# Linear attention in octets of heads: the first octet's K is loaded in two transfers of 48 and 80 rows instead of one of 128

## The chip, the cores and the metric

The kernel runs on one core of a Trainium2 chip. The metric is the time of one execution in device microseconds; the median of several runs counts. The core has a TensorE (PE, with its weight loads PEld), a VectorE (DVE), a ScalarE (ACT), a GpSimd (POOL) and a SyncE (SP), and 16 DMA engines that all queues share.

## The reference

Eight batches of twelve heads make 96 heads, each with 512 positions of 64 numbers in float32. For each head:

```python
Q_feat = np.maximum(0, Q)
K_feat = np.maximum(0, K)
KV = np.einsum('bhkd,bhkv->bhdv', K_feat, V)
K_sum = np.sum(K_feat, axis=2)
numerator = np.einsum('bhqd,bhdv->bhqv', Q_feat, KV)
denominator = np.einsum('bhqd,bhd->bhq', Q_feat, K_sum)
return numerator / (denominator[:, :, :, None] + 1e-10)
```

## The kernel before, in words

The 96 heads are handled in 12 octets of eight heads. An octet of Q, of K or of V is 1 MiB of float32, seen as 128 rows (SBUF partitions) of 2048 numbers: 8 KiB of one row of SBUF are 8 KiB in one piece in memory, and 16 rows hold one head.

**Loads.** From octet 1 on (and for Q from octet 0), POOL's queue issues the loads (`load`, L171 to L175), and they turn float32 into bf16 on the way. Six input slots (`NI`) are used in turn, most loads take two octets at once (`load_two`, L177), and six semaphores ("lanes") are taken in turn, so that a load's issue waits until the load six before it has landed. The K and V of octet 0 are loaded differently: SP's queue issues them at the very start, without a cast, into the output buffers `o_sb[0]` and `o_sb[1]` (L265 to L267), which are free until the outputs of octets 8 and 9 come. `kv_src` (L166) gives the source and the key on which the readers wait.

**Set-up.** While these loads run, POOL issues four loads, then sets an identity and the ones and zeros in `vo` and `mask` with 28 small memsets (L262), and after these issues the loads of octets 2 to 5. DVE makes the masks (L296 to L301), and then waits for octet 0's K: `prep_k` (L187 to L192) applies the ReLU and a mask in two instructions over all 128 rows. `prep_v` (L194) does V on ACT and DVE; TensorE can start on the sums of octet 0 after that.

**Steady state.** For each octet TensorE transposes Q, multiplies with the sums of the octet before, sums K times V for the next, and transposes the results; ACT and DVE move data between. The order on each engine is written out by hand in `step` (L341); `Order.op` (L58) finds out from reads and writes which semaphores an instruction must wait for, and puts the waits ahead of it.

**Stores.** An octet's result lies in one of ten output buffers. SP's queue stores them (`store`, L248), twelve transfers of 1 MiB, all held until the K of the last octet has landed (`keys.append(("k", (NO - 1) % NI))`). So the loads have the DMA engines first, and the stores after them. The kernel is over when the last store has landed.

The lines around the change:

```python
for c, X in enumerate((Kr, Vr)):
    do.op("sp", lambda e: e.dma_start(out=o_sb[c].rearrange("p r d -> p (r d)"), in_=X[0]),
          writes=[("o", c)], dma=lane("sp"))
load("q", 0)
```

Of the kernel before, what the change touches and what calls it, by code (L numbers as in the profile page):

```python
# [96 lines left out]
def kernel(  # L97
# [8 lines left out]
    B, H, S, D = Q.shape  # L106
    assert D == 64
    P = 128
# [8 lines left out]
    NI = 6  # L117
    NOUT = 10
    LANES = 6
# [16 lines left out]
    mask = sb.tile([P, 2, 2], fp32, name="mask")  # L136
    mask_h = sb.tile([P, 8, 2], fp32, name="mask_h")
    kf = sb.tile([P, RQ, 2, D], bf16, name="kf")
    vo = sb.tile([P, RQ, 2, D4], bf16, name="vo")
# [7 lines left out]
    rec = sb.tile([P, RQ], fp32, name="rec")  # L147
    ins = {n: sb.tile([P, NI, RQ * D], bf16, name=f"{n}_sb") for n in "qkv"}
    o_sb = [sb.tile([P, RQ, D], fp32, name=f"o_sb{i}") for i in range(NOUT)]
# [3 lines left out]
    ps_x = [psum.tile([P, 1024], fp32, name=f"ps_x{j}") for j in range(2)]  # L153

    names = ["dve", "act", "pool", "pe", "q2", "a0", "d0", "d1", "rq", "ev", "t0", "t1", "n0", "n1"]
    lanes = {"pool": [f"gl{i}" for i in range(LANES)], "sp": [f"sl{i}" for i in range(3)], "last": ["el"]}
    sems = {n: tc.alloc_semaphore("s_" + n) for n in names + sum(lanes.values(), [])}
    turn = {n: 0 for n in lanes}

    def lane(who):  # L160
        turn[who] += 1
        return lanes[who][(turn[who] - 1) % len(lanes[who])]

    do = Order(nc, sems)

    def kv_src(o):  # L166
        if o == 0:
            return (o_sb[0], ("o", 0)), (o_sb[1], ("o", 1))
        return [(ins[n][:, o % NI].rearrange("p (r d) -> p r d", d=D), (n, o % NI)) for n in "kv"]

    def load(n, *octets):  # L171
        o, i, m = octets[0], octets[0] % NI, len(octets)
        src = {"q": Qr, "k": Kr, "v": Vr}[n][o:o + m].rearrange("n p f -> p n f")
        do.op("pool", lambda e: e.dma_start(out=ins[n][:, i:i + m], in_=src, single_packet=True),  # L174
              writes=[(n, x % NI) for x in octets], dma=lane("pool"))  # L175

    def load_two(o):  # L177
        if o < NO - 2:
            load("q", o, o + 1)
            load("k", o, o + 1)  # L180
            load("v", o, o + 1)
        else:
            for x in (o, o + 1):
                for n in "kqv":
                    load(n, x)

    def prep_k(o, s, halves=(0, 1), after=()):  # L187
        src, key = kv_src(o)[0]
        rs = slice(R * halves[0], R * halves[-1] + R)
        do.op("dve", lambda e: e.tensor_scalar(kf[:, rs, s, :], src[:, rs], scalar1=0.0, scalar2=mask[:, 0, s:s + 1],  # L190
                                               op0=Alu.max, op1=Alu.mult),
              reads=[key, ("mask", 0), *after], writes=[("kf", s, j) for j in halves])  # L192

    def prep_v(o, t, halves, who, sem=None):  # L194
        src, key = kv_src(o)[1]
        rs = slice(R * halves[0], R * halves[-1] + R)
        to, src, m = vo[:, rs, t, 2:D + 2], src[:, rs], mask[:, 1, t:t + 1]
        if who == "act":
            make = lambda e: e.activation(to, src, Act.Copy, scale=m)  # L199
        else:  # L200
            make = lambda e: e.tensor_scalar(to, src, scalar1=m, scalar2=None, op0=Alu.mult)  # L201
        do.op(who, make, reads=[key, ("mask", 1), "vo1"], writes=[("vo", t, j) for j in halves], sem=sem)

    def copy_q(o):
        do.op("dve", lambda e: e.tensor_copy(q2.rearrange("p u f -> p (u f)"), ins["q"][:, o % NI]),  # L205
# [35 lines left out]
    def norm(o, j):  # L241
        i = (o + 2) % NOUT
        rs = slice(16 * j, 16 * j + 16)
        do.op("dve", lambda e: e.tensor_tensor(o_sb[i][:, rs], ps_x[j].rearrange("p (r d) -> p r d", d=D),  # L244
                                               rec[:, rs].unsqueeze(2).to_broadcast([P, 16, D]), op=Alu.mult),
              reads=[("x", j), "rec"], writes=[("o", i, j)] if i > 1 else [("o", i, j), ("o", i)], sem=f"n{j}")

    def store(o):  # L248
        i = (o + 2) % NOUT
# [11 lines left out]
    def memset(who, ap, value, key):  # L261
        do.op(who, lambda e: e.memset(ap, value), writes=[key] if isinstance(key, (str, tuple)) else key)  # L262

    def body():
        for c, X in enumerate((Kr, Vr)):  # L265
            do.op("sp", lambda e: e.dma_start(out=o_sb[c].rearrange("p r d -> p (r d)"), in_=X[0]),
                  writes=[("o", c)], dma=lane("sp"))  # L267
        load("q", 0)
        memset("pool", ident, 0.0, "ident")
        do.op("pool", lambda e: e.affine_select(out=ident, in_=ident, compare_op=Alu.not_equal, fill=1.0, base=0,  # L270
                                                pattern=[[-1, P]], channel_multiplier=1),
              reads=["ident"], writes=["ident"])
        for n in "kqv":
            load(n, 1)
        ones = vo[:, :, :, 1:D4 - 1]
        for c in range(4):
            memset("pool", ones[:, 8 * c:8 * c + 8, :, 0:D + 2:D1], 0.0, "vo1")
        for h in range(4):
            for c in range(4):
                memset("pool", ones[32 * h:32 * h + 32, 8 * c:8 * c + 8, h % 2, 0:D + 2:D1], 1.0, "vo1")  # L280
        for h in range(4):
            for t in range(2):
                memset("pool", mask[32 * h:32 * h + 32, 1, t:t + 1], 1.0 if h % 2 == t else 0.0,
                       [("m", h, t), ("mask", 1)])
        setup()
        load_two(2)
        load_two(4)
        begin()
        for o in range(NO):
            step(o)  # L290
        for n in lanes["pool"] + lanes["sp"]:
            nc.gpsimd.wait_ge(sems[n], do.count[n])
        nc.gpsimd.drain()

    def setup():
        do.op("dve", lambda e: e.tensor_copy(ident32, ident), reads=["ident"], writes=["ident32"])  # L296
        for c in range(2):
            do.op("dve", lambda e: e.tensor_reduce(
                out=mask_h[:, :, c], in_=ident32.rearrange("p (h b) -> p h b", h=8), op=Alu.add,
                axis=mybir.AxisListType.X), reads=["ident32"], writes=[("mh", c), "mask_h"])  # L300
        do.op("dve", lambda e: e.tensor_reduce(  # L301
            out=mask[:, 0, :], in_=mask_h[:, :, 0].rearrange("p (a s) -> p s a", s=2), op=Alu.add,
            axis=mybir.AxisListType.X), reads=["mask_h"], writes=[("mask", 0)])
        prep_k(0, 0)
        prep_k(0, 1)
        prep_v(0, 1, (0,), "act", "a0")
        prep_v(0, 0, (0, 1), "dve", "d0")
        prep_v(0, 1, (1,), "dve", "d1")
        do.op("dve", lambda e: e.memset(kvf.bitcast(fp32)[:, 0:4 * D1], 0.0), writes=KVD, sem="n0")
        do.op("dve", lambda e: e.memset(kvf.bitcast(fp32)[:, 4 * D1:], 0.0), writes=KVD, sem="n1")  # L310
        copy_q(0)
        for who, e, names in (("act", nc.scalar, ("t0", "t1", "rq", "ev")), ("dve", nc.vector, ("n0", "n1"))):
            for n in names:
                e.sem_inc(sems[n], 1)
                do.note(who, who, (), (), n, 1)
# [16 lines left out]
    def begin():  # L332
        transposed(1)
        relu_q(0)
        relu_q(1)
        summed(1)
        evac_kv()
        prep_v(1, 1, (0,), "act", "a0")
        prepare(1)

    def step(i):  # L341
        r = i + 2
        more, two = i + 1 < NO, i + 2 < NO

        if more:
            transposed(r)
        do.looped([("ev", r)], [*QT, *KVD], ["pd"])
        own_sums()
        if more:
            prep_v(i + 1, 0, (0, 1), "dve", "d0")  # L350
            prep_v(i + 1, 1, (1,), "dve", "d1")
        reciprocals()
        for j in range(2):
            do.looped([(f"n{j}", r)], [*QT, *KVD], [("x", j)])
        copy_ot(0, "act")
        copy_ot(1, "act" if more else "dve")
        if more:
            relu_q(0)
            relu_q(1)
            summed(r)  # L360
            evac_kv()
        if two:
            prep_v(i + 2, 1, (0,), "act", "a0")
            prepare(i + 2)
        do.looped([("t0", r), ("t1", r)], [*OT, "ident32"], [("x", 0)])
        do.looped([], [*OT, "ident32"], [("x", 1)])
        for j in range(2):
            norm(i, j)
        if i % 2 == 0 and i + 6 < NO:
            load_two(i + 6)  # L370
            if i + 8 == NO:
                for x in range(i):
                    store(x)
        if i + 8 >= NO:
            store(i)
# [50 lines left out]
    with tc.tile_critical(no_gpsimd_drain=True):  # L426
        body()
        products()
# [34 lines left out]
```

## Time and profile before

| | us |
|---|---|
| median of 3 runs (125.06 to 125.29) | 125.1 |
| the profiled execution's own time | 125.21 |
| its span, first to last instruction | 123.4 |
| SP issues octet 0's K (386 ns) | 0.96 |
| SP issues octet 0's V (425 ns) | 1.40 |
| DVE's first ReLU on K starts | 7.47 |
| DVE's first V scaling starts | 12.38 |
| the first store is issued | 87.63 |
| the last normalization ends, the last store is issued at | 112.37, 112.39 |

Engine shares of the span: PE 66%, PEld 59%, DVE 69%, ACT 62%, POOL 18%. DMA is the mean busy share of the 16 engines; a share above 1 in a window is two queues' packets that overlap on one engine. Each DMA also sends one 4-byte packet per engine to its semaphore; these are the packets "under 512 B" in the page.

### The profile page before, as it was taken

What the parts mean: (1) busy time and instruction counts of PE and PEld (TensorE: products, weight loads), DVE (VectorE), ACT (ScalarE), POOL (GpSimd) and SP (SyncE); (2) the same over time, 40 slices, a digit from 0 to 9 for tenths busy, and PEclk for the clock granted to TensorE, in tenths of its full rate; (3) what the DMA queues carried; (4) which work ended last, traced back from release to release, by engine and by line L of the source; (5) the groups of instructions that cost most, each with busy time, mean ns of one, the idle gap of its engine ahead of it and who ended that gap; (6) DMA issues with size and microseconds to landing.
All of it is one profiled execution on the core that took longest, in us unless ns stands there. A gap on an engine that the chain in (4) does not pass through costs nothing.

```text
span 123.4 us, 3445 instructions
## 1 busy us (share of the span) xinstructions
PE 81.2 (66%) x1440; PEld 72.4 (59%) x1440; DVE 85.7 (69%) x149; ACT 76.2 (62%) x108; POOL 21.6 (18%) x56
## 2 busy tenths in 40 slices
PE   0000088793579999898959889597999989390000
PEld 0000077693269789797939789495978977290000
DVE  1252936626975999999989899898999956733000
ACT  0000755991099697999859995799999896300000
POOL 5887922102022022010110110200000000000000
PEclk9999999999756999999999999999999999959555
DMA  2999999999999999999999999999999999999990
GB/s 72 393 313 234 212 214 214 212 212 216 216 212 215 215 216 214 212 216 214 212 215 215 215 215 214 214 215 214 212 324 421 425 425 427 422 425 425 430 425 35
DMA packets 6724, 32.55 MB, mean 264 GB/s; under 512 B 576, under 2 KB 576, under 8 KB 4928
## 3 DMA queue, kind: packets, MB, share of 16 engines
q0 software_dynamic: 4704, 17.83, 71.8%
q1 hardware_dynamic: 2016, 14.68, 28.5%
q8 instruction: 1, 0.02, 0.1%
q14 instruction: 3, 0.02, 0.0%
HBM read 37.75 MB, written 12.58 MB: 408 GB/s over the span
## 4 chain that ended last, share of the span: by engine, by line
DMA 43%; DVE 11%; PE 11%; POOL 11%; issue 9%; ACT 5%; POOLq 0%; DVEq 0%; SPq 0%
DMA v_sb<-in_V_dram 24%; DMA q_sb<-in_Q_dram 20%; DVE o_sb L244 7%; PE ps_x L421 5%; PE ps_kv L412 5%; POOL vo L262 5%; POOL q_sb L174 2%; POOL k_sb L174 2%; DVE vo L201 2%; ACT ot_sb L225 2%; ACT qt L209 1%; DVE own L230 1%; ACT kvd L217 1%; POOL v_sb L174 1%; ACT vo L199 1%
## 5 line engine op out<-in xcount | busy, mean ns | idle before, releaser
L244 DVE TENSOR_TENSOR o_sb<-ps_x,rec 128x1024 f32<-128x1024 f32 x24 | 28.5, 1219 | 5.6 <-PE ps_x L421 5.1
L412 PE MATMUL ps_kv<-vo,kf 64*128 64x132 bf16 x768 | 26.9, 229 | 7.0 <-ACT vo L199 3.5
L412 PEld LDWEIGHTS ps_kv<-vo,kf 64*128 64x128 bf16 x768 | 24.9, 99 | 10.2 <-ACT vo L199 7.8
L421 PE MATMUL ps_x<-ident,ot_sb 128*128 128x128 f32 x192 | 25.4, 289 | 1.7 <-DVE ot_sb L225 1.7
L209 ACT ACTIVATE qt<-ps_qt 128x1024 bf16<-128x1024 bf16 x24 | 23.5, 1040 | 2.1 <-PE ps_qt L388 2.1
L421 PEld LDWEIGHTS ps_x<-ident,ot_sb 128*128 128x128 f32 x192 | 22.6, 149 | 3.3 <-issue 2.2
L388 PE MATMUL ps_qt<-ident,q 128*128 128x128 bf16 x192 | 13.5, 226 | 16.2 <-DVE q L205 15.9
L225 ACT COPY ot_sb<-ps_x 128x1024 f32<-128x1024 f32 x23 | 22.2, 1015 | 2.9 <-PE ps_x L381 2.6
L190 DVE TENSOR_SCALAR kf<-k_sb,mask 128x1024 bf16<-128x1024 bf16 x44 | 19.2, 491 | 6.0 <-DMA k_sb<-in_K_dram 3.5
L388 PEld LDWEIGHTS ps_qt<-ident,q 128*128 128x128 bf16 x192 | 12.2, 101 | 16.5 <-issue 16.3
L217 ACT CAST kvd<-ps_kv 64x260 bf16<-64x260 f32 x48 | 18.0, 375 | 2.2 <-PE ps_kv L412 1.4
L199 ACT ACTIVATE vo<-v_sb,mask 128x1024 bf16<-128x1024 bf16 x11 | 12.7, 1154 | 10.1 <-DMA v_sb<-in_V_dram 9.9
L381 PE MATMUL ps_x<-qt,kvd 128*128 128x256 bf16 x96 | 13.7, 281 | 3.7 <-DVE o_sb L244 3.7
L201 DVE TENSOR_SCALAR vo<-v_sb,mask 128x2048 bf16<-128x2048 bf16 (+1 forms) x22 | 12.6, 617 | 1.3 <-DMA v_sb<-in_V_dram 1.3
L381 PEld LDWEIGHTS ps_x<-qt,kvd 128*128 128x128 bf16 x96 | 8.0, 99 | 6.2 <-DVE o_sb L244 5.0
L205 DVE COPY q<-q_sb 128x2048 bf16<-128x2048 bf16 x12 | 8.1, 674 | 2.1 <-PE ps_qt L388 2.1
L199 ACT ACT_TABLE_LOAD x1 | 1.3, 1283 | 12.4 <-DMA o_sb<-in_V_dram 12.4
L174 POOL DMA_DIRECT2D q_sb<-in_Q_dram x8 | 5.2, 655 | 18.1 <-DMA k_sb<-in_K_dram 8.7
L174 POOL DMA_DIRECT2D k_sb<-in_K_dram x7 | 5.0, 713 | 18.4 <-DMA q_sb<-in_Q_dram 10.1
L174 POOL DMA_DIRECT2D v_sb<-in_V_dram x7 | 4.8, 679 | 19.1 <-DMA v_sb<-in_V_dram 14.5
L381 PE MATMUL ps_kv<-kvd,qt 128*128 128x16 bf16 x192 | 7.0, 179 | 1.3 <-ACT kvd L217 1.3
L381 PEld LDWEIGHTS ps_kv<-kvd,qt 128*128 128x128 bf16 x192 | 6.1, 96 | 2.2 <-ACT kvd L217 2.1
(20 smaller groups left out, 29.5 us busy)
## 6 DMA issues: line engine op xcount, KB each, us to landing
out_dram<-o_sb SPq DMA_DIRECT2D x12, 1024.0 KB, 15.2
q_sb<-in_Q_dram POOLq DMA_DIRECT2D x4, 1024.0 KB, 26.6
k_sb<-in_K_dram POOLq DMA_DIRECT2D x4, 1024.0 KB, 27.9
v_sb<-in_V_dram POOLq DMA_DIRECT2D x4, 1024.0 KB, 29.1
q_sb<-in_Q_dram POOLq DMA_DIRECT2D x4, 512.0 KB, 15.2
k_sb<-in_K_dram POOLq DMA_DIRECT2D x3, 512.0 KB, 19.3
v_sb<-in_V_dram POOLq DMA_DIRECT2D x3, 512.0 KB, 15.5
o_sb<-in_K_dram SPq DMA_DIRECT2D x1, 1024.0 KB, 6.4
```

The lines of the kernel that those rows point to most:

```text
L174: do.op("pool", lambda e: e.dma_start(out=ins[n][:, i:i + m], in_=src, single_packet=True), writes=[(n, x % NI) for x in octets], dma=lane ...
L190: do.op("dve", lambda e: e.tensor_scalar(kf[:, rs, s, :], src[:, rs], scalar1=0.0, scalar2=mask[:, 0, s:s + 1], op0=Alu.max, op1=Alu.mult) ...
L199: make = lambda e: e.activation(to, src, Act.Copy, scale=m)
L201: make = lambda e: e.tensor_scalar(to, src, scalar1=m, scalar2=None, op0=Alu.mult)
L209: do.op("act", lambda e: e.activation(qt[:, j * (U // 2):(j + 1) * (U // 2)], ps_qt[j], Act.Relu), reads=[("pq", j)], writes=[("qt", j)], ...
L217: do.op("act", lambda e: e.copy(kvd[64 * c:64 * c + 64, s:8:2, c * D1:c * D1 + D1].rearrange("p (g t) d -> p g t d", t=2), ps_kv[64 * s:64 ...
L225: do.op(who, lambda e: e.copy(to, src) if who == "act" else e.tensor_copy(to, src), reads=[("x", j)], writes=[("ot", j)], sem=f"t{j}")
L244: do.op("dve", lambda e: e.tensor_tensor(o_sb[i][:, rs], ps_x[j].rearrange("p (r d) -> p r d", d=D), rec[:, rs].unsqueeze(2).to_broadcast( ...
L381: return pe.matmul(out_, lhsT, rhs, start=True, stop=True, skip_group_check=True)
L388: x = pe.transpose(ps_qt[u // 8][:, u % 8, :], q2[:, u, :], ident)
L412: x = pe.matmul(ps_kv[:, h, 0:2 * (D + 2)].rearrange("p (t d) -> p t d", t=2), kf[ps, R * g + k, :, :].rearrange("p s d -> p (s d)"), vo[p ...
L421: x = pe.transpose(ps_x[u // 8][:, u % 8 * P:u % 8 * P + P], ot[:, u].rearrange("p h c -> p (h c)"), ident32)
```

## The change

SP's queue gets three transfers at the start instead of two: rows 0 to 47 of octet 0's K, rows 48 to 127 of it, and V as before. Each has a lane of its own, so SP's lanes grow from three to four. The readers of this K (`prep_k` for octet 0) wait for both pieces: their instructions still cover all 128 rows. Octet 8's normalization, which later writes the same buffer, takes the two keys in place of the one. The order of instructions on TensorE, DVE, ACT and POOL is the same as before; SP has one transfer more.

```diff
-    lanes = {"pool": [f"gl{i}" for i in range(LANES)], "sp": [f"sl{i}" for i in range(3)], "last": ["el"]}
+    lanes = {"pool": [f"gl{i}" for i in range(LANES)], "sp": [f"sl{i}" for i in range(4)], "last": ["el"]}
...
+    FIRST = [[("o", c, rows) for rows in (((0, 48), (48, P)), ((0, P),))[c]] for c in range(2)]
+
     def kv_src(o):
         if o == 0:
-            return (o_sb[0], ("o", 0)), (o_sb[1], ("o", 1))
+            return [(o_sb[c], FIRST[c]) for c in range(2)]
...
     def prep_k(o, s, halves=(0, 1), after=()):
-        src, key = kv_src(o)[0]
+        src, keys = kv_src(o)[0]
...
-              reads=[key, ("mask", 0), *after], writes=[("kf", s, j) for j in halves])
+              reads=[*keys, ("mask", 0), *after], writes=[("kf", s, j) for j in halves])
...
-              reads=[("x", j), "rec"], writes=[("o", i, j)] if i > 1 else [("o", i, j), ("o", i)], sem=f"n{j}")
+              reads=[("x", j), "rec"], writes=[("o", i, j)] if i > 1 else [("o", i, j), *FIRST[i]], sem=f"n{j}")
...
         for c, X in enumerate((Kr, Vr)):
-            do.op("sp", lambda e: e.dma_start(out=o_sb[c].rearrange("p r d -> p (r d)"), in_=X[0]),
-                  writes=[("o", c)], dma=lane("sp"))
+            for key in FIRST[c]:
+                ps = slice(*key[2])
+                do.op("sp", lambda e: e.dma_start(out=o_sb[c][ps].rearrange("p r d -> p (r d)"), in_=X[0][ps]),
+                      writes=[key], dma=lane("sp"))
```

More of the change, by code (lines that the diff above doesn't have):

```diff
@@ L164 @@
     do = Order(nc, sems)
+    FIRST = [[("o", c, rows) for rows in (((0, 48), (48, P)), ((0, P),))[c]] for c in range(2)]
     def kv_src(o):
         if o == 0:
-            return (o_sb[0], ("o", 0)), (o_sb[1], ("o", 1))
-        return [(ins[n][:, o % NI].rearrange("p (r d) -> p r d", d=D), (n, o % NI)) for n in "kv"]
+            return [(o_sb[c], FIRST[c]) for c in range(2)]
+        return [(ins[n][:, o % NI].rearrange("p (r d) -> p r d", d=D), [(n, o % NI)]) for n in "kv"]
     def load(n, *octets):
@@ L191, in prep_k @@
                                                op0=Alu.max, op1=Alu.mult),
-              reads=[key, ("mask", 0), *after], writes=[("kf", s, j) for j in halves])
+              reads=[*keys, ("mask", 0), *after], writes=[("kf", s, j) for j in halves])
     def prep_v(o, t, halves, who, sem=None):
-        src, key = kv_src(o)[1]
+        src, keys = kv_src(o)[1]
         rs = slice(R * halves[0], R * halves[-1] + R)
@@ L201, in prep_v @@
             make = lambda e: e.tensor_scalar(to, src, scalar1=m, scalar2=None, op0=Alu.mult)
-        do.op(who, make, reads=[key, ("mask", 1), "vo1"], writes=[("vo", t, j) for j in halves], sem=sem)
+        do.op(who, make, reads=[*keys, ("mask", 1), "vo1"], writes=[("vo", t, j) for j in halves], sem=sem)
     def copy_q(o):
```

## The prediction

> **What bounds the kernel now.** I read the slices of the span first, then the DMA queues, then the windows of the first microseconds and of the end, then the issues of SP.
>
> The slices show which resource never rests:
>
> ```profile
> PE   0000088793579999898959889597999989390000
> DVE  1252936626975999999989899898999956733000
> DMA  2999999999999999999999999999999999999990
> GB/s 72 393 313 234 212 214 214 212 212 216 216 212 215 215 216 214 212 216 214 212 215 215 215 215 214 214 215 214 212 324 421 425 425 427 422 425 425 430 425 35
> ```
>
> The DMA engines are busy from the second slice to the last but one, while PE and DVE have holes at both ends. The loads count their bf16 output (214 GB/s), the stores their float32 (425); an engine works equally hard in both. So the end is about the moment at which the engines start, plus the work queued for them, plus what happens after the last packet. The windows show the two ends:
>
> ```profile
> 0.00:2.00 2.00, 0.00 (x0) 0.00 (x0) 0.00 (x0) 0.00 (x0) 0.76 (x5) 1.00 0.07 8
> 2.00:3.00 1.00, 0.00 (x0) 0.00 (x0) 0.23 (x2) 0.00 (x0) 0.92 (x4) 1.00 0.54 188
> 3.00:4.00 1.00, 0.00 (x0) 0.00 (x0) 0.73 (x3) 0.00 (x0) 1.00 (x3) 1.00 0.97 410
> 4.00:5.00 1.00, 0.00 (x0) 0.00 (x0) 0.00 (x0) 0.00 (x0) 0.89 (x4) 1.00 1.00 410
> ...
> 120.00:123.40 3.40, 0.00 (x0) 0.00 (x0) 0.00 (x0) 0.00 (x0) 0.00 (x0) 0.50 0.18 75
> ```
>
> The last two columns are DMA share and GB/s. Octet 0's K is what fills the engines here: idle to 2 us, half busy to 3, full after. The packets of the trace say it closer: four engines begin their first K packet at 1.98 to 2.09 us but end it at about 3.0, eight begin at 2.58 to 2.67, four at 2.81 to 2.94. A time lost or won by every engine here has no later idle time to vanish in. At the end, fourteen engines send their last packet between 120.3 and 121.2 us and two at 121.7 and 122.0; these two set the end, with up to 1.6 us of slack for the others.
>
> ```profile
> 0.96 0.39 SPq L266 DMA_DIRECT2D o_sb<-in_K_dram  x1
> 1.40 0.42 SPq L266 DMA_DIRECT2D o_sb<-in_V_dram  x1
> ...
> q0 software_dynamic: 4704, 17.83, 71.8%
> q1 hardware_dynamic: 2016, 14.68, 28.5%
> ```
>
> SP's issues take about 0.4 us each. SP's queue q1 has 2016 packets for 14 transfers: 16 of each are semaphore packets, 1792 carry 8 KiB, that is 8 per engine and transfer. 28.5% of 16 x 123.4 us over 1792 is 0.314 us for a packet; in the trace most take 0.309.
>
> Compute does not set the end: the last normalization is over at 112.37 us, and the last store then waits behind others until 122. That store's own packets need 2.5 us (8 x 0.309) of an engine, and the first engine is done at 120.3, so compute could be some 5 us later (120.3 - 2.5 - 112.4) before an engine ran dry.
>
> **The change part by part.**
>
> *One more issue on SP.* It costs SP about 0.4 us, so V is issued at some 1.8 instead of 1.40 us. V's packets aren't wanted before K's are done (the engines leave K at 5.03 to 5.35 us in the trace), and K took 1.0 us from issue to first packet, so V would be ready by 2.8. Cost 0; without that cover 0.4 us. POOL's first load (1.46 us) is on another queue and moves by nothing.
>
> *Sixteen more semaphore packets*, one per engine, 9 ns each in the trace: +0.01 us.
>
> *One more wait on DVE* before the first ReLU. Queued behind it are the ReLUs, DVE's share of V and the first copy of Q; TensorE waits for them. DVE idles 3.7 us there anyway, and the instruction still needs all 128 rows, so the early 48 rows start no compute. If K lands later, compute starts later by as much, and the 5 us above cover it. POOL is touched by this too: two of its memsets take 1.16 instead of 0.17 us while DVE's ReLUs run (7.47 to 9.95 us), and they stand ahead of POOL's loads at 11.85. But POOL then waits 1.64 us for a landing before its load at 16.87, and the engines have work queued throughout, so a shift there is worth 0 as well, up to 2 us either way without that queue.
>
> *The start of the engines.* The first transfer now has 3 packets per engine instead of 8, and if the late starters (2.81 to 2.94) wait for descriptors of a long transfer, they could start with the first group or the second. No row shows a shorter first transfer. Bounds: nothing, or the 0.3 us between 2.6 and 2.9 for the four last, up to 0.6 us (1.98 against 2.6) if all are released as early as the first four. Since those four had no data before the others, I hold 0.3 us for the most, and take 0.
>
> *How the packets run.* In a 128-row transfer the sixteen engines write to 128 rows; now they write to 48 neighbouring rows, then to 80. The trace has 128-row transfers alone. If the way into SBUF isn't divided by rows, each engine has 3 + 5 = 8 packets of 0.309 us as before: cost 0. If it is divided, so that a transfer's rate goes with the part of the rows that it reaches, 48 rows get 3/8 of the rate and 80 rows 5/8, and each piece takes as long as the whole did: 8 x 0.309 = 2.47 us. K then holds the engines 4.94 instead of 2.47 us, +2.47. Between them: engines that are done with their three packets go on to their five in the other rows, so that the pieces overlap by a part. The end goes by the slowest engines, not the mean, so I stand nearer the upper end: two thirds of 2.47, +1.6 us. This is the only term of size, and the one that I am least sure of. The packet of 0.309 us is the row it goes by, as nothing in the trace lets two engines write one group of rows.
>
> On this term the Trainium skill speaks against the change. "SBUF — State Buffer", section "Door 1: The DMA port swizzle", says that the partition number picks one of 16 ports, that partitions 0 to 63 all lie on eight of them and 64 to 127 on the other eight, and measures 196 GB/s for 64 partitions against 328 for 128, at 1 MiB. An estimate from that page: 48 rows (0.39 MB) take 2.0 instead of 1.2 us, the 64 rows of the other half (0.52 MB) 2.7 instead of 1.6, together +1.9 us, and the sum would be 127.0. No transfer in this trace is narrow enough to show it.
>
> Sum: +1.6 + 0.01 + 0 + 0 = +1.6 us on the profiled 125.21, which lies 0.1 above the median. On the median: 125.1 + 1.6 = 126.7 us.
>
> **The rivals.**
>
> *Forecast: the engines collide*, 126.0 to 127.7 (0.9 us, where the slack of fourteen engines at the end hides a part, to the whole 2.47 and a little of chance). For it: nothing is idle behind, so any loss stays. Against it: no narrow transfer in the trace.
>
> *Faster: the short first transfer starts the engines sooner*, and they don't collide. For it: the starts are spread over 0.9 us and the share is only 0.54 from 2 to 3 us; the DMA-bound remainder would hand a gain through to the end. Against it: the four earliest packets ended no sooner than the others, as if the data were late and not the descriptors. It gains 0.3 us, 124.8; it decides where the collision costs under 0.3 us per engine.
>
> *No change*: eight packets per engine either way, in the same order, 9 ns of semaphores. That is 125.1. For it: no engine's work grows, and DVE still needs both pieces. It is also the case in which the change doesn't do what it says, because the same engines carry the same packets in the same order.
>
> *A little slower, without collision*: q0's first packets come at 5.35 us, just after K. With a boundary after the third packet, Q's could be let in there, and K's last five alternate with Q's: K lands 5 x 0.31 = 1.5 us later. The engines lose nothing by it, and compute has the room; only a start of the sums that is late enough to delay stores would cost. Some 0.3 us, 125.4, if the cover fails.
>
> **How the numbers follow.** About 0.2% (0.25 us) is what a measurement of this kernel can tell from no change. Collision 0.64, sooner start 0.22, no change 0.10, late K 0.04. Slower: 0.64 + 0.04 = 0.68; faster 0.22; same 0.10. The range goes from 124.7, which takes in the sooner start, to 127.7; about 0.05 is left out below and 0.1 above. The likeliest case's own range is 126.0 to 127.7.
>
> **What would show it.** If the engines collide, K's packets in the first 6 us take well over 0.309 us, the GB/s from 3 to 5 us fall from 410 towards half, the two pieces of K have landed later than the one did, DVE's first ReLU starts after 7.47 us, and everything from there to the last store is later by one and the same amount, at unchanged rates of 214 and 425 GB/s. If the start is won, the share in the window from 2 to 3 us rises from 0.54, with 410 GB/s after it. I am wrong on the main step if the rate from 3 to 5 us stays at 410 GB/s, and wrong on the bound if K is slower and the end is the same, since then the engines that set the end weren't touched.

## The result and the profile after

The change makes the kernel slower: 127.04 us (median of 6 runs, 126.55 to 127.52) against 125.19 (6 runs), a ratio of 1.0146 with a 95% interval of 1.0119 to 1.0173. That is +1.85 us where +1.6 was forecast. The profiled execution took 127.06 us with a span of 125.3.

The page's slices after, the same four as before:

```profile
PE   0000039889149989898997889598898989490000
DVE  1107453480985699999999989898999984943000
DMA  4999999999999999999999999999999999999990
GB/s 102 204 279 305 213 211 213 217 216 212 212 218 216 211 211 216 221 212 211 217 221 209 212 217 216 213 211 211 217 301 421 418 418 432 439 419 421 426 424 31
```

The engines are again busy from the start to the end, and the rates of the long stretches are the same, 214 and about 425 GB/s. What differs is the second and third slice (3.1 to 9.4 us): 204 and 279 GB/s where there were 393 and 313. The windows (the last two columns are DMA share and GB/s) place it:

```profile
2.00:3.00 1.00, 0.00 (x0) 0.00 (x0) 0.23 (x1) 0.00 (x0) 0.93 (x4) 1.00 1.09 279
3.00:4.00 1.00, 0.00 (x0) 0.00 (x0) 0.74 (x3) 0.00 (x0) 1.00 (x3) 1.00 1.05 172
4.00:5.00 1.00, 0.00 (x0) 0.00 (x0) 0.00 (x0) 0.00 (x0) 0.89 (x4) 1.00 1.00 221
5.00:9.00 4.00, 0.00 (x0) 0.00 (x0) 0.00 (x0) 0.00 (x0) 2.91 (x20) 1.00 1.00 252
20.00:90.00 70.00, 59.22 (x1113) 53.40 (x1110) 58.44 (x108) 56.04 (x81) 8.83 (x13) 0.95 1.06 214
```

A window counts a packet where it begins, with its whole length and all its bytes. So a share can be above 1 with only one queue at work, as in the first of these lines, and not only where two queues' packets overlap; and two neighbouring windows can differ by chance.

From 2 to 3 us the engines are busier than before (share 1.09 against 0.54) and move more (279 against 188 GB/s). From 3 to 5 us they are as busy as before and move half: 172 and 221 instead of 410 GB/s. (With a packet's bytes spread over the time that it took, it is 196 and 197 instead of 422 and 421.) A share of 1 at half of the rate is the mark of packets that last longer, not of packets that are missing. The packets of the trace say the same: the first 128 packets on SP's queue, nearly all of them K's, last 593 ns on average instead of 335, the first 48 of them (598) and the other 80 (590) alike.

SP's issues and the queues, from the timeline and the page:

```profile
0.96 0.86 SPq L270 DMA_DIRECT2D o_sb<-in_K_dram  x2
1.87 0.42 SPq L270 DMA_DIRECT2D o_sb<-in_V_dram  x1
...
q1 hardware_dynamic: 2032, 14.68, 29.8%
```

V is issued 0.47 us later; q1 has the 16 semaphore packets more. DVE's first instructions on octet 0 are late by 2.35 and 1.94 us:

```profile
9.82 2.48 DVE L192 TENSOR_SCALAR kf<-o_sb,mask 128x2048 bf16<-128x2048 f32 x2 [6.00 <-DMA o_sb<-in_K_dram]
14.32 1.95 DVE L203 TENSOR_SCALAR vo<-o_sb,mask 128x2048 bf16<-128x2048 f32 x2 [2.02 <-DMA o_sb<-in_V_dram]
```

The delay is made in the first microseconds and then carried: a transfer's semaphore arrivals (the median of its 16) are late by 1.72 us at the fourth load from the start, by 1.73 at the seventh, and by 1.87 us at the last store.

### The profile page after: what moved, and what is told of

Its sections match the earlier page's. It is cut to its first block, busy times and chain, and to the rows that moved or that the text cites. A ratio compares the mean times of both kernels' runs of the same rounds, so it can differ in the third digit from the quotient of the medians.

```text
span 125.3 us, 3447 instructions
## 1 busy us (share of the span) xinstructions
PE 81.3 (65%) x1440; PEld 72.7 (58%) x1440; DVE 85.0 (68%) x149; ACT 76.2 (61%) x108; POOL 20.8 (17%) x56
## 4 chain that ended last, share of the span: by engine, by line
DMA 57%; DVE 11%; PE 10%; issue 5%; ACT 5%; POOL 2%; POOLq 0%; DVEq 0%; SPq 0%
DMA v_sb<-in_V_dram 23%; DMA k_sb<-in_K_dram 21%; DMA q_sb<-in_Q_dram 12%; DVE o_sb L246 7%; PE ps_x L425 5%; PE ps_kv L416 5%; DVE vo L203 2%; ACT ot_sb L227 2%; ACT qt L211 1%; DVE own L232 1%; ACT kvd L219 1%; ACT vo L201 1%; DVE ot_sb L227 1%; POOL k_sb L176 1%; POOL q_sb L176 1%
## 5 line engine op out<-in xcount | busy, mean ns | idle before, releaser
L416 PE MATMUL ps_kv<-vo,kf 64*128 64x132 bf16 x768 | 27.5, 232 | 7.2 <-ACT vo L201 3.6
L416 PEld LDWEIGHTS ps_kv<-vo,kf 64*128 64x128 bf16 x768 | 25.5, 101 | 10.4 <-ACT vo L201 6.6
L176 POOL DMA_DIRECT2D q_sb<-in_Q_dram x8 | 6.1, 764 | 20.1 <-DMA k_sb<-in_K_dram 10.8
```

The source lines that it names most:

```text
L416: x = pe.matmul(ps_kv[:, h, 0:2 * (D + 2)].rearrange("p (t d) -> p t d", t=2), kf[ps, R * g + k, :, :].rearrange("p s d -> p (s d)"), vo[p ...
```

## The experiments

Times are medians, ratios are against runs of the kernel before on the same chip, with the 95% interval.

**1. The same bytes, cut by columns.** All 128 rows in each of the two transfers.

```diff
-                ps = slice(*key[2])
-                do.op("sp", lambda e: e.dma_start(out=o_sb[c][ps].rearrange("p r d -> p (r d)"), in_=X[0][ps]),
+                fs = slice(*key[2])
+                do.op("sp", lambda e: e.dma_start(out=o_sb[c].rearrange("p r d -> p (r d)")[:, fs], in_=X[0][:, fs]),
```

with (0, 768) and (768, 2048) for K.

> K again in two transfers of the same bytes as in the change (0.39 and 0.66 MB), but cut by columns: all 128 rows x 768 columns, then all 128 rows x 1280. Collision by rows: every transfer reaches all rows, so packets keep their rate (the 410 GB/s of the kernel before from 3 to 5 us), K lands as before or up to 0.3 us earlier, time 124.9 to 125.3. If it is the cutting itself that costs (a second transfer, its semaphores, the second wait): as the change, about 127.0, with 170 to 220 GB/s from 3 to 5 us.

125.97 us, ratio 1.0049 (1.0035 to 1.0063): between the two theories. The loss is less than half of the change's, but it isn't nothing. The windows show a cost of another kind:

```profile
2.00:3.00 1.00, 0.00 (x0) 0.00 (x0) 0.23 (x1) 0.00 (x0) 0.93 (x4) 1.00 0.97 203
3.00:4.00 1.00, 0.00 (x0) 0.00 (x0) 0.74 (x3) 0.00 (x0) 1.00 (x3) 1.00 0.71 182
4.00:5.00 1.00, 0.00 (x0) 0.00 (x0) 0.00 (x0) 0.00 (x0) 0.89 (x4) 1.00 1.06 416
```

Here the rate falls to 182 GB/s from 3 to 4 us, and after that the engines run at 416 GB/s, where the change is at 221. The packets of the trace place the loss inside the first piece: of its 128 packets of 3 KiB, over half last 0.12 to 0.145 us, but eight that begin between 2.7 and 3.2 us last 0.7 to 1.1 us, and its semaphore packets come at 3.6 to 4.6 us. The share of 0.71 from 3 to 4 us is no idle time: packets that began before 3 us fill it, and by their own times the engines are busy throughout. So the expectation of experiment 10, which speaks of engines that had run out of packets, misreads this share. This is another loss than the change's, at another place, so this run is no clean control. Experiments 3, 6 and 10 take it up.

**2 and 3. 64 rows at a time, neighbouring or spread.**

```diff
-(((0, 48), (48, P)), ((0, P),))[c]
+(((0, 64), (64, P)), ((0, P),))[c]          # 2: rows 0 to 63, then 64 to 127
+(((0, P, 2), (1, P, 2)), ((0, P),))[c]      # 3: even rows, then odd rows
```

> K cut at row 64: rows 0 to 63, then 64 to 127. Collision by rows, with half of the rate for half of the rows: K's 8 packets of 0.309 us per engine all double, 4.94 instead of 2.47 us, so the loss is as large as the change's or a little larger: 127.0 to 127.6. If the uneven cut (3 and 5 packets) is what costs, an even one of 4 and 4 is cheaper: 125.2 to 126.

> K cut into its even rows and its odd rows, 64 each, so each transfer has half of the rows, as the cut at 64, but spread over the whole width. Collision by groups of neighbouring rows: two engines can still meet in a group, but all groups are reached at all times once the engines have drifted apart: 125.2 to 126. If only the count of rows in a transfer matters: as the cut at 64, about 127.2.

The cut at 64: 126.47 us, ratio 1.0103 (1.0085 to 1.0121), less than the 127.0 to 127.6 expected. Even and odd rows: 125.59 us, ratio 1.0028 (1.0018 to 1.0039). Number, size and length of the transfers are equal, and SP issues both alike (1.19 and 1.18 us for the two); only the rows differ. K's packets last 522 ns in the one and 368 in the other, and the losses are 1.21 and 0.33 us. So it matters which rows a transfer holds. The windows of the cut at 64, then of the even and odd rows:

```profile
4.00:5.00 1.00, 0.00 (x0) 0.00 (x0) 0.00 (x0) 0.00 (x0) 0.89 (x4) 1.00 1.11 209
5.00:6.00 1.00, 0.00 (x0) 0.00 (x0) 0.00 (x0) 0.00 (x0) 0.71 (x6) 1.00 0.93 229
```

```profile
4.00:5.00 1.00, 0.00 (x0) 0.00 (x0) 0.00 (x0) 0.00 (x0) 0.89 (x4) 1.00 1.09 262
5.00:6.00 1.00, 0.00 (x0) 0.00 (x0) 0.00 (x0) 0.00 (x0) 0.71 (x6) 1.00 1.04 311
```

A part of this low rate is not loss: in both runs packets of Q's load (8 KiB read, 4 KiB written) begin from 4.2 or 4.3 us on, ahead of the second piece of K (5.23 and 5.14), while in the change they begin at 6.27. That they make the cut at 64 cheaper than the change (1.21 against 1.85 us) is possible, but no run shows it.

**4. Compute late, loads untouched.**

```diff
-        prep_k(0, 0)
+        prep_k(0, 0, after=[("o", 1)])
```

> The kernel before, with one change: DVE's first ReLU on octet 0's K also waits for octet 0's V, so that it starts at about 12.4 instead of 7.47 us and everything after it on DVE by about 2.5 us later; the loads are the same. If compute's delay is covered by the some 5 us in hand at the end: 125.0 to 125.4. If the late start of compute is what the change pays for: 127 or more.

125.2 us, ratio 0.9999 (0.9990 to 1.0008), although the ReLU starts 4.75 us later than in the kernel before, at 12.22:

```profile
12.22 2.48 DVE L190 TENSOR_SCALAR kf<-o_sb,mask 128x2048 bf16<-128x2048 f32 x2 [8.41 <-DMA o_sb<-in_V_dram]
14.62 2.11 DVE L201 TENSOR_SCALAR vo<-o_sb,mask 128x2048 bf16<-128x2048 f32 x2
```

The late ReLU of the change (2.35 us) is therefore worth nothing by itself. What is paid is the time of the DMA engines.

**5 and 6. Where the engines meet: memory or SBUF.** The cut at 64 with one side changed each time.

```diff
-in_=X[0][ps]),
+in_=X[0][ps] if c else X[0][key[2][0] // 64:P:2]),           # 5: K read from every second row of memory
-out=o_sb[c][ps]
+out=o_sb[c][ps if c else slice(key[2][0] // 64, P, 2)]       # 6: K written to every second row of SBUF
```

> The cut at row 64 with another source: K's even rows in memory go to rows 0 to 63 of SBUF, the odd ones to rows 64 to 127 (octet 0's K is thereby in another order, a change of the computation). Two transfers, 64 rows each, written as in the cut at 64, read as in the cut into even and odd rows. If the engines meet where they write in SBUF: as the cut at 64, about 126.5, with K's packets at some 520 ns on average. If they meet where they read in memory: as the cut into even and odd rows, about 125.6, packets some 370 ns.

> The counterpart: memory rows 0 to 63 of K go to the even rows of SBUF, 64 to 127 to the odd ones (K again in another order). Meeting in SBUF: about 125.6, packets some 370 ns. Meeting in memory: about 126.5, packets some 520 ns.

Neighbouring rows in SBUF, every second in memory: 127.38 us, ratio 1.0169 (1.0152 to 1.0186), K's packets 593 ns. Every second row in SBUF, neighbouring in memory: 125.32 us, ratio 1.0005 (0.9995 to 1.0014), packets 347 ns. (Both runs leave octet 0's rows of K in another order; they time the loads and are not kernels to keep.) The cost goes with the side that writes to SBUF, and it is gone when the 64 rows of a transfer are spread. The windows of the cut at 64, of experiment 5 and of experiment 6, in this order:

```profile
5.00:9.00 4.00, 0.00 (x0) 0.00 (x0) 0.00 (x0) 0.00 (x0) 2.91 (x20) 1.00 1.05 237
5.00:9.00 4.00, 0.00 (x0) 0.00 (x0) 0.00 (x0) 0.00 (x0) 2.91 (x20) 1.00 1.08 218
5.00:9.00 4.00, 0.00 (x0) 0.00 (x0) 0.00 (x0) 0.00 (x0) 2.91 (x20) 1.00 1.03 301
```

The semaphores say the same. From the start of a semaphore packet to its arrival, the median over K's engines is 0.34 us in the kernel before, and 0.33 to 0.34 us for both pieces of experiments 3 and 6. It is 1.20 and 0.83 us for the two pieces of the change, 1.04 and 0.78 for the cut at 64, and 1.16 and 0.69 for experiment 5.

Experiment 6 is also the clean control that experiment 1 was not. It has a third transfer, a second wait, and a K that is complete at 9.56 instead of 7.37 us, as in the change (9.69), and it costs nothing that can be measured. So neither a second transfer nor the late K is what the change pays for.

Reading every second row has a price of its own. It is the only difference between experiments 3 and 6 in how the pieces are moved (1.0028 against 1.0005, and the intervals do not overlap), and experiment 5 is dearer than the cut at 64 by 0.9 us, though both write alike and Q's packets start alike (4.41 and 4.28 us). Why, and why it is dearer together with the collision, is open.

**7. 32 and 96 rows.**

```diff
+(((0, 32), (32, P)), ((0, P),))[c]
```

> K cut into 32 and 96 rows. If a transfer's rate goes with the part of the rows that it reaches (the upper bound of the prediction), both pieces take as long as the whole: K's packets double, as in the cut at 48: 126.8 to 127.3. If 32 rows already run at half of the rate, as 64 do, the first piece loses 2 x 0.309 us per engine and the second about as much: loss 1.2 us, 126.2 to 126.6.

126.37 us, ratio 1.0092 (1.0068 to 1.0116): a loss of 1.11 us, as expected if 32 rows run at half of the rate, and not the 2.47 us of a rate that goes with the part of the rows. The first piece alone rules out a quarter of the rate. Its 0.26 MB would take 2.47 us at a quarter of 425 GB/s; its first packet begins at 2.24 us, and all its semaphore arrivals are in by 4.36 us. The windows of this run:

```profile
2.00:3.00 1.00, 0.00 (x0) 0.00 (x0) 0.23 (x1) 0.00 (x0) 0.93 (x4) 1.00 0.75 262
3.00:4.00 1.00, 0.00 (x0) 0.00 (x0) 0.74 (x3) 0.00 (x0) 1.00 (x3) 1.00 1.04 262
4.00:5.00 1.00, 0.00 (x0) 0.00 (x0) 0.00 (x0) 0.00 (x0) 0.89 (x4) 1.00 0.98 262
```

The first line is not a rate of the 32 rows: all 32 packets of their piece begin in it, and 32 x 8 KiB are 262 KB. The other two are the 96 rows, at 262 instead of 410 GB/s.

**8 and 9. V cut instead of K, and both.**

```diff
+(((0, P),), ((0, 48), (48, P)))[c]          # 8
+((0, 48), (48, P))                          # 9, and a fifth lane for SP
```

> K is whole again and octet 0's V is cut, 48 and 80 rows. If the cost is the collision of the transfer's packets wherever it stands in the queue: V's packets grow from 0.32 us to about 0.6, a loss near that of K's cut and without the earlier first packets: 126.5 to 127.5. If the cost belongs to the first transfer of the kernel (cold engines): 125.0 to 125.5.

> K and V of octet 0 both cut, 48 and 80 rows: twice the dose. If the engines are the bound from their first packet to their last, the losses of K's cut (1.85 us) and of V's cut (1.5) add up: 128.3 to 128.9. If a part of the first loss was hidden by slack, or compute's cover of some 5 us is used up (V then lands some 4 us later than in the kernel before, and more), the sum differs: under 127.8 if the two overlap, over 129.2 if compute becomes late too.

V cut: 126.78 us, ratio 1.0128 (1.0109 to 1.0147). K keeps its rate and the dip comes where V is:

```profile
3.00:4.00 1.00, 0.00 (x0) 0.00 (x0) 0.73 (x3) 0.00 (x0) 1.00 (x3) 1.00 1.02 418
4.00:5.00 1.00, 0.00 (x0) 0.00 (x0) 0.00 (x0) 0.00 (x0) 0.89 (x4) 1.00 0.97 410
5.00:6.00 1.00, 0.00 (x0) 0.00 (x0) 0.00 (x0) 0.00 (x0) 0.71 (x6) 1.00 1.21 369
6.00:7.00 1.00, 0.00 (x0) 0.00 (x0) 0.00 (x0) 0.00 (x0) 0.77 (x5) 1.00 1.07 184
```

V's packets last 515 instead of 322 ns, 8 x 0.193 = 1.54 us for each engine; the time grew by 1.52. Both cut: 128.91 us, ratio 1.0268 (1.0243 to 1.0294). The loss of 3.63 us is the sum of the two (1.85 + 1.52 = 3.37) within the spread of these runs (128.1 to 129.18). The cost isn't a matter of the first transfer, and nothing in the kernel absorbs it up to this size.

**10. Columns again, the large piece first.**

```diff
-(((0, 768), (768, RQ * D)), ((0, RQ * D),))[c]
+(((0, 1536), (1536, RQ * D)), ((0, RQ * D),))[c]
```

> K cut by columns with the large piece first: 128 rows x 1536, then x 512. In the cut at 768 columns the engines had run out of packets before the second piece's came (share 0.71 from 3 to 4 us). If that gap was the cost of 0.7 us, a first piece of twice the size covers it, and what is left is the earlier first packets: 124.8 to 125.3. If pieces of rows smaller than 8 KiB are what costs: 125.6 to 126.

125.55 us, ratio 1.0018 (1.0006 to 1.0029), between the two expectations. From 3 to 4 us the engines move 344 instead of 182 GB/s, and the loss is 0.27 instead of 0.71 us:

```profile
3.00:4.00 1.00, 0.00 (x0) 0.00 (x0) 0.73 (x3) 0.00 (x0) 1.00 (x3) 1.00 0.91 344
```

So the smaller rows as such are not what cost 0.7 us, as these 6 and 2 KiB packets show; but the sooner first packets brought no gain either. What holds single packets up in the first microseconds of these two runs is open. No cut that was tried beats one transfer of 128 rows.

## Why the prediction was right, point by point

**The bound.** That the DMA engines are the bound from the first packet to the last, so that a loss at the start stays, held: the delay at the fourth load (1.72 us) is still there at the last store (1.87), and doses add (experiment 9). The slack of fourteen engines at the end hid nothing, because all sixteen lost about the same: twelve end at 122.0 to 122.4 us instead of 120.3 to 120.7, the last at 123.95 instead of 121.99.

**How the packets run (+1.6 us).** The mechanism was right: neighbouring rows are a way into SBUF that the engines must share. The term was somewhat small: 8 x (593 - 335) ns = 2.07 us per engine. The reason given for the two thirds, that the slowest engines decide, wasn't needed; the mean engine lost that much. And the upper bound was reasoned wrongly: a rate that goes with the part of the rows would have made 32 and 96 rows cost the full 2.47 us, and they cost 1.11. What the runs bear out is groups of rows, of which 32 neighbouring rows reach well more than a quarter; their loss fits a half, as large a part as 64 rows reach. This is what the Trainium skill says in "SBUF — State Buffer", section "Door 1: The DMA port swizzle": 0 to 31 and 0 to 63 both lie on eight of 16 ports. The trace agrees, with 172 to 221 GB/s from 3 to 5 us (for 48 and 80 rows) against the page's 196 for 64 partitions, and the estimate by that page (127.0) lay nearer to 127.04 than the forecast. That it lay so near is in part luck: worked out in the same way from the page's two rates, an estimate for the cut at 64 is +2.15 us, and 1.21 were measured. Why K's packets last 593, 522 and 473 ns in the cuts at 48, 64 and 32 is open. Which engine writes which rows in these transfers no run here shows.

**The start of the engines (0 taken, 0.3 us at most).** Here the step was off by a little. The engines' first packets begin at 1.99 to 2.33 us instead of 1.98 to 2.90 (the prediction has 2.94, which is already a second packet's start), 0.40 us earlier on average, and end 0.23 us earlier. The rival of the sooner start may thus have had a part in it, one far smaller than the collision. With it the sum closes: +2.07 for K's packets, -0.40 for the start, +0.09 for V's packets (334 instead of 322 ns), +1.76 us against the measured 1.72 at the fourth load. That the short first transfer causes the sooner start isn't shown. In experiment 4, with unchanged loads, the first packets begin at 1.99 to 2.68 us, 0.21 us earlier on average than in the kernel before; they last longer for it (K's packets 369 instead of 335 ns on average), and the time is the same. So a part of the 2.07 and of the 0.40 can be the same waiting, counted once on each side.

That +1.6 lay so near to +1.85 is in part luck: by this sum the one term was too small by 0.47 us, and the start, taken at 0, gave 0.40 us back.

**The costs of nothing.** V's later issue was free: its packets follow K's. The wait on DVE and the late K were free (experiment 4). POOL moved as said: DVE's ReLUs now start after POOL's memsets of `vo`, which take 4.53 instead of 6.49 us, and POOL's first load after them is issued at 9.91 instead of 11.85 us; the engines had work queued, and nothing came of it.

**Q let in between the pieces.** It didn't happen in the change (Q's first packet is at 6.27 us, when K's second piece ends on the first engines); it did in the cut at 64.

## What to carry to other kernels

When the DMA engines have no idle time from start to end, a transfer's price is the time that its packets hold the engines, and its landing time hardly matters as long as compute has time in hand (here some 5 us). A load that is cut into neighbouring rows can run at about half of the rate while the engines look fully busy; look at GB/s beside the share, and at the packets where a window is short. If a load must be cut, cut it so that each piece reaches all groups of rows: by columns with a large first piece, or by every second row (here 0.27 and 0.33 us instead of 1.1 to 1.9).

## What was not expected of the hardware

- Two transfers of 64 neighbouring rows of SBUF cost 1.2 us (2.1 with every second row of memory as source), and two of 64 rows into every second row nothing that can be measured (1.0005, 0.9995 to 1.0014; 0.33 us with every second row of memory as source).
- SP takes some 0.59 us to issue a transfer of 64 rows, for neighbouring rows and for every second one, and 0.39 to 0.43 for 32, 48, 80, 96 or 128 rows. V's issue of 128 rows behind the two of 64 also took 0.59.
- One engine has a packet of 16 KiB of queue q8 ("instruction" in the page) among K's packets, 1.02 us long before and 1.48 after. It makes that engine the last of K's sixteen, at 7.37 us where fifteen are in by 5.70 (9.69 and 8.19 after), so DVE waits for it. Experiment 4 says that this wait costs nothing either.
